# A transformer layer on one core: room of the dynamic-DMA scratch given to pages, and the copies back of the mLSTM outputs split in two

## The chip, the core and the metric

The kernel runs on one core of a Trainium2 chip. The core has a matrix engine (TensorE, in the profile PE, its weight loads PEld), a vector engine (VectorE, DVE), a scalar engine (ScalarE, ACT), GpSimd (POOL) and a sync engine (SP), which here only issues DMAs. Each engine runs its own instructions in the order in which they stand in its program; semaphores hold an instruction until what it needs is done. DMAs issued by SP and by POOL are carried out by the same 16 DMA engines. SBUF is the on-chip memory that DMAs fill and engines read; PSUM holds what PE accumulates.

The metric is the time of one execution on the device in microseconds, the median of several.

## The reference

One layer on x of 256 positions by 2048 channels: a SwiGLU feed-forward block, a mixer, a second SwiGLU block, each followed by a residual and a layer norm, then a gated embedding.

```python
x = layer_norm(ALPHA*x + 0.5*swiglu(x, ffn1_w1, ffn1_w3, ffn1_w2))        # 2048 -> 5632 -> 2048
proj = x @ w_in                                                            # 2048 x 11272
mq, mk, mv, mo, mi, mf, sq, sk, sv, ga, gb = split(proj)
y_m  = head_norm(mlstm(conv(mq), conv(mk), mv, mi, mf)) * sigmoid(mo)      # 4 heads of 256
y_sb = stick_breaking(sq, sk, sv)                                          # 8 heads of 128
merged = sigmoid(ga)*(y_m @ w_up_m) + sigmoid(gb)*(y_sb @ w_up_sb)
x = layer_norm(ALPHA*x + merged @ w_out)
x = layer_norm(ALPHA*x + 0.5*swiglu(x, ffn2_w1, ffn2_w3, ffn2_w2))
x = x + sigmoid(x @ w_ple_gate) * (p @ w_ple_proj)
```

All is float32. The weights are read once from DRAM, in blocks of 256 rows by 512 columns (0.5 MB).

## The kernel before

**Weights and units.** A block of weights is loaded from DRAM into a *raw* page (`loads`, the DMA at L1143, issued by SP). ACT then rounds it to a high part (L1170) and DVE forms the low part as the difference (L1174); both are *split* pages. A *unit* of the program multiplies one split weight with one of the two halves (t) of 128 positions: six matmuls, which are three (L1221, high by high; L1222, high by low; L1223, low by high) for each 128 rows. The left operand is an `actT` tile, activations transposed and split in the same way, one page for a chunk c of 512 channels and a half t. Some pairs of products (SwiGLU's two up-projections, the mixer's gates) are formed by `seven`, which saves one product in eight by sums of weights. Such sums are made by POOL, as DMAs that add a second block into a raw page (L337), or by DVE (L342), which needs both blocks landed. The tiles `seeded` are the PSUM banks of these products.

**Pages.** Raw blocks, splits, `actT` tiles and larger intermediates (`big`, `qk`) all live in one pool of 44 pages of 4,096 bytes per partition. A page is handed out in the order of the program; the instruction that fills it waits until the last use of what was in it is done. How far loads run ahead is limited by `limits`: in the feed-forward blocks by the count of pages in use, in the mixer by `room` (raw pages, splits), which entries of the program made by `rooms(raw, splits)` set as it goes on. The rest of SBUF is taken by constants, the residual, temporaries, and a scratch for the descriptors of dynamic DMAs, whose size the kernel leaves at its default.

**Order.** The program is a list of units and of calls, written out once; side work (transposes, softmax-like chains, normalisations) is spawned with a due time counted in matmuls, so it does not depend on pages. In the mixer, `main` (the projections q, k, v, the stick-breaking columns, then the up-projections `ups(g, 0)`) is woven with the units of the gates by `weave`. SP's queue holds all loads of weights in the order of first use, and between them the copies of the kept residual, the norms' rows, the copies back below and the outputs.

**The mLSTM outputs.** When a head pair is done, its `actT` pages (chunk c, half t) are written to DRAM by POOL (`away`, L804) and their pages given free. `back` fetches all four into new pages, by four DMAs on SP (L813). It stands in `main` four units before its end at that time, that is before the last four of the sixteen units of 256 columns which close the projections; the units of `ups(0, 0)`, from the weight `w_up_m`, come next. Of these, the first four units (two blocks of 256 rows, two halves) read chunk 0 and the next four chunk 1, with units of the gates between them.

Of the kernel before, what the change touches and what calls it, by code (L numbers as in the profile page):

```python
# [8 lines left out]
F32 = mybir.dt.float32  # L9
# [6 lines left out]
TT = S // P  # L16
# [6 lines left out]
EPS = 1e-5  # L23
COL = 512

PAGES = 44
TEMP_BUFS = 6
FORMED = 8
SPARE = 2
# [142 lines left out]
def flat(pairs):  # L172
    return [u for p in pairs for u in p]
# [7 lines left out]
def kernel(  # L181
# [6 lines left out]
    nc = tc.nc  # L188
    x, out = x[0], out[0]
# [4 lines left out]
    res_pool = ctx.enter_context(tc.tile_pool(name="res", bufs=1))  # L194
    page_pool = ctx.enter_context(tc.tile_pool(name="page", bufs=PAGES))
    temp_pool = ctx.enter_context(tc.tile_pool(name="temp", bufs=TEMP_BUFS))
# [11 lines left out]
    def temp():  # L208
        sched.until(lambda: temps[0] < TEMP_BUFS)
        temps[0] += 1  # L210
        return temp_pool.tile([P, COL], F32, name="temp", tag="temp")

    def drop(n=1):
        temps[0] -= n

    def misc(shape):
        return ps_pool.tile(shape, F32, name="ms", tag="ps")
# [6 lines left out]
    def act_tile():  # L224
        pages[0] += 1
        return page_pool.tile([P, 2, 4, P], F32R, name="actT", tag="page")
# [84 lines left out]
    def group(w, rows, col0, cols, act, done):  # L311

        accs = [{} for _ in range(TT)]
        pairs = []
        for i, r in enumerate(rows):
            tile = plain(rows_of(w, r, col0, cols))
            pairs.append([Unit(tile, t, accs[t], act, r // COL, r % COL // P,
                               i == 0, i == len(rows) - 1, done) for t in range(TT)])
        return pairs
# [68 lines left out]
    program = []  # L388

    def rooms(*n):  # L390
        return lambda: room.__setitem__(slice(0, len(n)), n)
# [5 lines left out]
    class Norm:  # L397
# [23 lines left out]
        def columns(self, raw, n):  # L421
            ps = misc([P, 2 * n])
            nc.tensor.transpose(ps[:], raw[0:2 * n, 0:P], ident[0:2 * n, 0:2 * n])
            self.gb = small.tile([P, 2, n], F32, name="gb", tag="gb", bufs=1)
            nc.vector.tensor_copy(out=self.gb[:], in_=ps.rearrange("q (a c) -> q a c", c=n))
            drop()
            return
            yield
# [307 lines left out]
    def qk_done(which, g):  # L736
        stage = {}

        def done(ps, t):
            stage[t] = temp()  # L740
            nc.scalar.copy(stage[t][:], ps)
            if t == TT - 1:
                sched.spawn(conv(which, g, stage), DELAY["cv0"])
        return done

    def conv(which, g, stage):
        yield from wait("cw")
        for e in range(2):
            h = 2 * g + e
            ps = misc([P, 2, S])  # L750
            for k in range(2):
                for t in range(TT):
                    nc.tensor.transpose(ps[:, k, t * P:(t + 1) * P],
                                        stage[t][:, (2 * e + k) * P:(2 * e + k + 1) * P], ident[:])
            if ("qk", h) not in st:
                st["qk", h] = page_pool.tile([P, 2, 2, S], F32, name="qk", tag="page")
            acc = temp().rearrange("q (k s) -> q k s", s=S)
            w = lambda k, j: st["cw"][:, j * 16 + 8 * which + 2 * h + k:j * 16 + 8 * which + 2 * h + k + 1]
            for k in range(2):
                activate(acc[:, k], ps[:, k], ACT.Copy, scale=w(k, 3))  # L760
            for k in range(2):
                for j in range(3):
                    d = 3 - j
                    nc.vector.scalar_tensor_tensor(out=acc[:, k, d:], in0=ps[:, k, :S - d], scalar=w(k, j),
                                                   in1=acc[:, k, d:], op0=ALU.mult, op1=ALU.add)
            yield DELAY["cv1"]
            activate(st["qk", h][:, which], acc[:], ACT.Silu)
            drop()
            flags.add(("qk", which, h))
            yield DELAY["cv2"]  # L770
        drop(2)
# [28 lines left out]
    ymT, ysbT = ActT(act_tile), ActT(act_tile)  # L800
    aside = {(c, t): dram_pool.tile([P, 2, 4, P], F32, name=f"aside{c}{t}") for c in range(2) for t in range(TT)}
# [4 lines left out]
        return  # L806
        yield

    def back():
        for c in range(2):  # L810
            for t in range(TT):
                ymT.tiles[c, t] = act_tile()
                nc.sync.dma_start(out=ymT.tiles[c, t][:].bitcast(F32), in_=aside[c, t][:])  # L813

    def diag(tl):
        return tl[:, 0:512].rearrange("q (a s) -> q a s", s=S)[:, :, 0:P]
# [104 lines left out]
    def in_sequence(gens):  # L921
        for g in gens:
            yield from g
            yield DELAY["m2"]
# [4 lines left out]
    head = group(w_in, range(0, D, 2 * P), 0, COL, x1T, qk_done(0, 0))  # L929
    program.extend(skewed(head[:SKEW]) + flat(head[SKEW:]))  # L930
    program.extend(columns(4096, 2 * HM + 2 * DS, gates_done))
    main = [rooms(13, 4)] + columns(1024, COL, qk_done(1, 0)) + [rooms(8)]
    main += columns(COL, COL, qk_done(0, 1)) + [load_norm_m, rooms(8)] + columns(1024 + COL, COL, qk_done(1, 1)) + [rooms(8)]
    for g in range(2):
        main += columns(2048 + g * COL, COL, v_done(g))
        main.append(lambda g=g: sched.spawn(in_sequence([mlstm(2 * g), mlstm(2 * g + 1)])))
    for first, n in ((2, 4), (8, 4), (16, 4), (12, 4), (20, 4), (6, 2)):
        main += columns(sq0 + first * DS, n * DS, lambda ps, t, f=first, n=n: sb_columns(ps, t, f, n))
        if first in (2, 20):
            main.insert(len(main) - (0 if first == 2 else 6), rooms(11 if first == 2 else 7))  # L940
        if first == 16:
            main.append(rooms(10))
            main.append(lambda: [sched.spawn(in_sequence([stick(a), stick(a + 2), stick(a + 4), stick(a + 6)]))
                                 for a in (0, 1)])

# [64 lines left out]
    def ups(g, half):  # L1010
        if half:
            return flat(group(w_up_sb, range(0, HS * DS, 2 * P), g * COL, COL, ysbT, up_done(g, 1)))
        return flat(group(w_up_m, range(0, HM * DM, 2 * P), g * COL, COL, ymT, up_done(g, 0)))

    main[len(main) - 4:len(main) - 4] = [back]
    for g in range(3):
        main += ups(g, 0) + [rooms(12)]
    program.extend(weave(main, chained([sigmoid7(w_in[:, 3072:], w_in[:, 3072 + COL:], 0, mo_place, mo_after)] + [gates7(g) for g in range(4)])))
    program.append(rooms(10, 6))
    for g in range(3):  # L1020
        program.extend(ups(g, 1))
    program.append(lambda: sched.spawn(refill(), DELAY["mt"]))
# [97 lines left out]
    def mixing():  # L1120
        j = pos["split"]
        return held[0] or any(-EDGE <= j - e < EDGE for e, _ in edges) or [m for e, m in edges if e <= j][-1:] == [True]
# [13 lines left out]
    def loads(most=len(raws)):  # L1136
        while (pos["load"] < most and pos["raw"] < (4 if pos["at"] < 6 else limits(pos["split"])[0])
               and (mixing() or pages[0] + pos["raw"] + 2 * max(limits(pos["split"])[1], len(splits)) < PAGES - SPARE)):
            j = pos["load"]
# [63 lines left out]
    for u in program:  # L1203
# [14 lines left out]
        for k in range(2):  # L1218
            hi, lo = a[:, 0, u.sub + k], a[:, 1, u.sub + k]
            first, last = u.start and k == 0, u.stop and k == 1  # L1220
# [40 lines left out]
```

## Time and profile before

| | |
|---|---|
| runs shown | 2203.69, 2204.67, 2205.21 us; median 2204.67 |
| the profiled execution | 2203.56 us, of which its span is 2201.9 |
| instructions in the span | 27807 |
| moved by DMA | 531.26 MB, mean 241 GB/s |
| granted TensorE clock, mean | 0.998 |

The span goes from the first to the last instruction of the program. The profile's page gives the busy time of each engine; its views give, for an engine or a stretch of time, the instructions in order, what ended the idle time before them, and who waited for whom. In a row of the timeline stand the start, the duration, the engine, the line of the code, the operation, the tile that is written and those that are read, and in brackets the idle time just before it with what ended that. Names with a q (SPq) are queues: their rows are the issue of a DMA. A matmul's duration overlaps the next one's, so the distance of two starts is what one costs.

### The profile page before, as it was taken

Reading aid. Unit: us, or ns where it says so; the run is one execution under the profiler, and the core shown is the slowest. Engines: PE = TensorE matmul, PEld = TensorE weight load, DVE = VectorE, ACT = ScalarE, POOL = GpSimd, SP = SyncE. Lnnn points to the kernel's source line nnn. Section 1 sums busy time; section 2 is a strip of 40 time slices with the busy share of each in tenths; the row PEclk is TensorE's granted clock in tenths of the full one; section 3 lists DMA queues with packets and bytes.
Section 4 is the critical chain, followed back from the end, with each engine's and each line's share of the span. In section 5 each row is a group of like instructions: output and inputs, shape, how many; then the busy total and the mean of one; then the engine's idle time right before and its main releaser. Section 6 shows DMA issues by size and latency. Waiting matters only on the chain.

```text
span 2201.9 us, 27807 instructions
## 1 busy us (share of the span) xinstructions
PE 2174.7 (99%) x9948; PEld 1797.7 (82%) x9948; DVE 1811.6 (82%) x1993; ACT 1345.6 (61%) x1615; POOL 242.1 (11%) x209
## 2 busy tenths in 40 slices
PE   9999999999999999999998999999999999999999
PEld 7888888888887888878886788888888888888878
DVE  6889988888898798778675877599898989889884
ACT  6556555666575666666766544556665666666562
POOL 3111001110100101011111100011011101110000
PEclk9999999999999999999999999999999999999999
DMA  9899889987993869798777876679879998999652
GB/s 347 222 254 269 255 240 303 267 246 213 287 327 116 242 186 254 216 249 262 200 212 212 301 264 196 214 167 314 260 225 248 305 258 247 245 275 302 213 166 72
DMA packets 276523, 531.26 MB, mean 241 GB/s; under 512 B 16768, under 2 KB 25888, under 8 KB 276128
## 3 DMA queue, kind: packets, MB, share of 16 engines
q1 hardware_dynamic: 229824, 437.20, 58.7%
q0 software_dynamic: 46560, 92.29, 23.0%
q8 instruction: 78, 1.28, 0.2%
q14 instruction: 61, 0.50, 0.1%
HBM read 523.12 MB, written 6.29 MB: 240 GB/s over the span
## 4 chain that ended last, share of the span: by engine, by line
PE 93%; DVE 3%; ACT 2%; issue 1%; DMA 1%; POOL 0%; DVEq 0%; ACTq 0%; POOLq 0%
PE mm L1222 25%; PE mm L1223 25%; PE mm L1221 25%; PE seeded L1222 5%; PE seeded L1221 5%; PE seeded L1223 5%; DVE split L1174 2%; PE ms L267 1%; ACT split L1170 1%; DMA actT<-aside 1%; ACT temp L239 1%; PE ms L456 0%; PE ms L848 0%; PE ms L836 0%; DVE raw L342 0%
## 5 line engine op out<-in xcount | busy, mean ns | idle before, releaser
L1174 DVE TENSOR_TENSOR split<-raw,split 128x1024 fp32r<-128x1024 f32 (+2 forms) x1073 | 1255.0, 1204 | 201.8 <-ACT split L1170 188.2
L1170 ACT CAST split<-raw 128x1024 fp32r<-128x1024 f32 (+2 forms) x1073 | 1079.2, 1038 | 463.6 <-PE mm L1222 114.8
L1221 PE MATMUL mm<-split,actT 128*128 128x512 f32 (+2 forms) x2608 | 1014.7, 389 | 9.5 <-DMA actT<-aside 6.7
L1222 PE MATMUL mm<-split,actT 128*128 128x512 f32 (+2 forms) x2608 | 1003.8, 385 | 7.2 <-DVE split L1174 7.1
L1223 PE MATMUL mm<-split,actT 128*128 128x512 f32 (+2 forms) x2608 | 1003.5, 385 | 2.3 <-DVE actT L272 2.3
L1222 PEld LDWEIGHTS mm<-split,actT 128*128 128x128 f32 x2608 | 490.7, 188 | 105.9 <-DVE split L1174 12.3
L1221 PEld LDWEIGHTS mm<-split,actT 128*128 128x128 f32 x2608 | 490.6, 188 | 105.8 <-issue 7.9
L1223 PEld LDWEIGHTS mm<-split,actT 128*128 128x128 f32 x2608 | 490.2, 188 | 100.6 <-DVE actT L272 3.1
L337 POOL DMA_DIRECT2D raw<-in_ffn_w_dram x128 | 154.7, 1216 | 1172.1 <-DVE split L1174 1016.5
L342 DVE TENSOR_TENSOR raw<-raw 128x1024 f32<-128x1024 f32 x168 | 204.6, 1218 | 22.2 <-DMA raw<-in_w_in_dram 11.7
L1221 PE MATMUL seeded<-split,actT 128*128 128x512 f32 x504 | 198.8, 394 | 0.0
L1222 PE MATMUL seeded<-split,actT 128*128 128x512 f32 x504 | 197.2, 391 | 0.2 <-DVE split L1174 0.2
L1223 PE MATMUL seeded<-split,actT 128*128 128x512 f32 x504 | 196.7, 390 | 0.0
L571 DVE SCALAR_TENSOR_TENSOR xres<-mm,xres 128x512 f32<-128x512 f32 x160 | 108.7, 684 | 22.4 <-PE mm L1223 22.4
L1222 PEld LDWEIGHTS seeded<-split,actT 128*128 128x128 f32 x504 | 95.0, 188 | 20.6 <-DVE split L1174 1.6
L1223 PEld LDWEIGHTS seeded<-split,actT 128*128 128x128 f32 x504 | 94.9, 188 | 19.8
L1221 PEld LDWEIGHTS seeded<-split,actT 128*128 128x128 f32 x504 | 95.0, 188 | 19.4 <-issue 0.3
L269 ACT CAST actT<-ms 128x512 fp32r<-128x512 f32 x60 | 35.2, 587 | 83.7 <-PE ms L267 83.7
L337 POOL DMA_DIRECT2D raw<-in_w_in_dram x40 | 48.9, 1227 | 304.1 <-DVE split L1174 241.6
L272 DVE TENSOR_TENSOR actT<-ms,actT 128x512 fp32r<-128x512 f32 x60 | 41.1, 685 | 24.2 <-ACT actT L269 15.1
L239 ACT ACTIVATE temp<-mm 128x512 f32<-128x512 f32 (+1 forms) x38 | 21.8, 574 | 57.9 <-PE mm L1223 57.9
L235 ACT ACT_TABLE_LOAD x36 | 46.2, 1283 | 0.6
(153 smaller groups left out, 714.5 us busy)
## 6 DMA issues: line engine op xcount, KB each, us to landing
raw<-in_ffn_w_dram SPq DMA_DIRECT2D x527, 512.0 KB, 8.2
raw<-in_w_in_dram SPq DMA_DIRECT2D x168, 512.0 KB, 5.4
raw<-in_ffn_w_dram POOLq DMA_DIRECT2D x128, 512.0 KB, 9.5
raw<-in_w_in_dram POOLq DMA_DIRECT2D x40, 512.0 KB, 8.5
raw<-in_w_out_dram SPq DMA_DIRECT2D x32, 512.0 KB, 4.9
raw<-in_w_ple_gate_dram SPq DMA_DIRECT2D x24, 512.0 KB, 4.9
raw<-in_w_up_m_dram SPq DMA_DIRECT2D x16, 512.0 KB, 5.7
raw<-in_w_up_sb_dram SPq DMA_DIRECT2D x16, 512.0 KB, 5.8
```

What stands on the lines that cost most here:

```text
L235: nc.scalar.preload_act_table_set(table[0])
L239: nc.scalar.activation(out, in_, func, **kw)
L269: nc.scalar.copy(dst[:, 0], ps[:])
L272: nc.vector.tensor_tensor(out=dst[:, 1], in0=ps[:], in1=dst[:, 0], op=ALU.subtract)
L337: nc.gpsimd.dma_start(out=raw.tile[:, :, :cols], in_=src.src, accum_op=ALU.add)
L342: nc.vector.tensor_tensor(out=a.tile[:, :, :cols], in0=a.tile[:, :, :cols], in1=b.tile[:, :, :cols], op=ALU.add)
L571: nc.vector.scalar_tensor_tensor(out=xs, in0=ps, scalar=0.5, in1=xs, op0=ALU.mult, op1=ALU.add)
L1170: nc.scalar.copy(hi[:, ks], r[:, ks])
L1174: nc.vector.tensor_tensor(out=lo[:, ks], in0=r[:, ks], in1=hi[:, ks], op=ALU.subtract)
L1221: nc.tensor.matmul(ps, hi, w[0][:, k, :u.cols], start=first, stop=False, skip_group_check=u.onto)
L1222: nc.tensor.matmul(ps, hi, w[1][:, k, :u.cols], start=False, stop=False, skip_group_check=u.onto)
L1223: nc.tensor.matmul(ps, lo, w[0][:, k, :u.cols], start=False, stop=last, skip_group_check=u.onto)
```

## The change

The scratch of dynamic DMAs is set to 4,096 bytes per partition, and the pool gets three pages of 4,096 bytes more. In the mixer the limits on raw pages rise: 13 to 15, 8 to 12 (twice), 8 to 11, 11 to 14, 10 to 13, 7 to 10, 12 to 15, and at its end 10 to 12. `back` fetches one chunk: chunk 0 seven units before the end of the projections, chunk 1 two units before it.

```diff
-PAGES = 44
+PAGES = 47
...
-    def back():
-        for c in range(2):
-            for t in range(TT):
-                ymT.tiles[c, t] = act_tile()
-                nc.sync.dma_start(out=ymT.tiles[c, t][:].bitcast(F32), in_=aside[c, t][:])
+    def back(c):
+        for t in range(TT):
+            ymT.tiles[c, t] = act_tile()
+            nc.sync.dma_start(out=ymT.tiles[c, t][:].bitcast(F32), in_=aside[c, t][:])
...
-    main = [rooms(13, 4)] + columns(1024, COL, qk_done(1, 0)) + [rooms(8)]
-    main += columns(COL, COL, qk_done(0, 1)) + [load_norm_m, rooms(8)] + columns(1024 + COL, COL, qk_done(1, 1)) + [rooms(8)]
+    main = [rooms(15, 4)] + columns(1024, COL, qk_done(1, 0)) + [rooms(12)]
+    main += columns(COL, COL, qk_done(0, 1)) + [load_norm_m, rooms(12)] + columns(1024 + COL, COL, qk_done(1, 1)) + [rooms(11)]
...
-            main.insert(len(main) - (0 if first == 2 else 6), rooms(11 if first == 2 else 7))
+            main.insert(len(main) - (0 if first == 2 else 6), rooms(14 if first == 2 else 10))
...
-            main.append(rooms(10))
+            main.append(rooms(13))
...
-    main[len(main) - 4:len(main) - 4] = [back]
+    for c, ahead in ((1, 2), (0, 8)):
+        main.insert(len(main) - ahead, lambda c=c: back(c))
     for g in range(3):
-        main += ups(g, 0) + [rooms(12)]
+        main += ups(g, 0) + [rooms(15)]
...
-    program.append(rooms(10, 6))
+    program.append(rooms(12, 6))
...
-    nc = bacc.Bacc("TRN2", target_bir_lowering=False, num_devices=1)
+    nc = bacc.Bacc("TRN2", target_bir_lowering=False, num_devices=1, dynamic_dma_scratch_size=4096)
```

The order of the instructions of PE, ACT, DVE and POOL is the same before and after, but for line numbers, which move by one. What moves is SP's queue. First the place where the rows of the mLSTM head norm (`in_norm_m`, L783) are loaded, among the loads of the input projection (x34 are 34 rows alike in a row):

```order
 L1143 DMA raw<-in_w_in_dram 128x2x512 x3
 L1143 DMA raw<-in_w_in_dram 128x2x264 x8
-L1143 DMA raw<-in_w_in_dram 128x2x512 x30
+L1143 DMA raw<-in_w_in_dram 128x2x512 x34
 L783 DMA big<-in_norm_m_dram 128x1024
-L1143 DMA raw<-in_w_in_dram 128x2x512 x114
+L1143 DMA raw<-in_w_in_dram 128x2x512 x110
```

Four loads of weights have moved ahead of that DMA, which itself stands at the same point of the program. Second, SP's queue around the copies back; `aside_94` and `aside_95` are the two halves of chunk 0, `aside_96` and `aside_97` those of chunk 1:

```order
 L1143 DMA raw<-in_w_up_m_dram 128x2x512 x3
 L1143 DMA raw<-in_w_in_dram 128x2x512
-L813 DMA actT<-aside_94 128x1024
-L813 DMA actT<-aside_95 128x1024
-L813 DMA actT<-aside_96 128x1024
-L813 DMA actT<-aside_97 128x1024
+L812 DMA actT<-aside_94 128x1024
+L812 DMA actT<-aside_95 128x1024
 L1143 DMA raw<-in_w_in_dram 128x2x512
 L1143 DMA raw<-in_w_up_m_dram 128x2x512 x2
+L812 DMA actT<-aside_96 128x1024
+L812 DMA actT<-aside_97 128x1024
```

Chunk 0's copies keep their place among the loads; chunk 1's now stand behind one more load of `w_in` and two more of `w_up_m`.

## The prediction

> **What bounds the kernel now.** First the busy times of the engines and the waits of the matrix engine (PE).
>
> ```profile
> PE 2174.7 (99%) x9948; PEld 1797.7 (82%) x9948; DVE 1811.6 (82%) x1993; ACT 1345.6 (61%) x1615; POOL 242.1 (11%) x209
> PE mm L1222 <- DVE split L1174: 7.1, 10, 1.1
> PE mm L1221 <- DMA actT<-aside: 6.7, 1, 6.7
> PE mm L1221 <- ACT big L1077: 2.4, 3, 1.5
> ```
>
> PE is busy for 2174.7 us of a span of 2201.9, so at most some 27 us can be had in all; an edit pays only where PE stands still or runs slowly. The last three rows give the wait in total, how often, and the longest: the ten waits for a split weight are short, and a single one, for an mLSTM output copied back from DRAM, takes 6.7 us. Next, the stretches around that wait (us from the start; then PE, PEld, DVE, ACT and POOL busy; granted clock, DMA share, GB/s).
>
> ```profile
> 1150.00:1160.00 10.00, 9.47 (x55) 7.85 (x53) 6.96 (x9) 5.99 (x9) 0.79 (x1) 1.00 0.49 131
> 1160.00:1170.00 10.00, 9.24 (x52) 7.83 (x52) 7.97 (x10) 9.08 (x12) 5.42 (x6) 1.00 0.76 144
> 1170.00:1180.00 10.00, 6.77 (x46) 5.96 (x44) 5.67 (x6) 5.28 (x8) 0.67 (x1) 1.00 1.09 255
> 1180.00:1190.00 10.00, 6.50 (x18) 5.20 (x19) 2.52 (x6) 2.37 (x4) 0.00 (x0) 0.66 0.63 237
> ```
>
> PE loses time in two ways: it waits, and from 1180 to 1190 its clock is granted at 0.66 only. The DMA engines are half idle before 1160 and full after 1170. The timelines of PE and of SP's queue there (start, duration, instruction, idle time before it and what ended that):
>
> ```profile
> 1175.95 0.82 PE L913 MATMUL ms<-temp,big 128*128 128x256 f32 x4
> 1183.50 0.76 PE L1221 MATMUL mm<-split,actT 128*128 128x512 f32 x1 [6.73 <-DMA actT<-aside]
> ...
> 1184.92 0.63 PE L1221 MATMUL mm<-split,actT 128*128 128x512 f32 x1
> 1185.34 0.63 PE L1222 MATMUL mm<-split,actT 128*128 128x512 f32 x1
> ...
> 1188.64 0.39 PE L1221 MATMUL mm<-split,actT 128*128 128x512 f32 x1
> 1188.87 0.39 PE L1222 MATMUL mm<-split,actT 128*128 128x512 f32 x1
> ...
> 1192.07 0.39 PE L1222 MATMUL mm<-split,actT 128*128 128x512 f32 x1
> ...
> 1196.53 0.47 PE L1221 MATMUL mm<-split,actT 128*128 128x512 f32 x1
> ```
> ```profile
> 1161.37 5.70 SPq L1143 DMA_DIRECT2D raw<-in_w_up_m_dram  x3
> 1170.45 0.37 SPq L1143 DMA_DIRECT2D raw<-in_w_in_dram  x1
> 1170.86 2.26 SPq L813 DMA_DIRECT2D actT<-aside  x4
> DMA to landing us min/median/max: 12.5/12.8/13.1
> ```
>
> PE is done with all else at 1176.77 (1175.95 + 0.82). The four copies back were issued only from 1170.86 on, and took 12.5 to 13.1 us to land. After the wait matmuls start 0.43 us apart, from 1188.64 on 0.23 apart: the twelve from 1183.50 to 1188.64 took 5.14 us instead of 12 x 0.23 = 2.76, so **2.4 us** were lost to the clock.
>
> **The change, part by part.** The sum is made against the profiled execution: 2203.56 us, of which 2201.9 are its span and 1.7 lie around it. It is 1.1 under the median of the three runs, 2204.67.
>
> *First pair of copies.* Three more pages, with the mixer's limits on raw pages raised by 2 to 4, let each load take the page release that served the load about three places earlier. So the w_in load ahead of the copies (1170.45) moves to about the release of 1161.37, three loads back. The first two copies follow on the next two releases, which are those of the second and third up_m load (by 1167.07, the end of that row). Issue is then 1161.4 to 1167.1, against 1170.86. Landing is bounded by the nearest rows, the up_m loads and the copies themselves:
>
> ```profile
> raw<-in_w_up_m_dram SPq DMA_DIRECT2D x6, 512.0 KB, 4.7
> raw<-in_w_in_dram POOLq DMA_DIRECT2D x4, 512.0 KB, 10.3
> ```
>
> With 4.7 us they are there by 1171.8 at the latest; with 13.1 between 1174.5 and 1180.2, and a wait of up to 3.4 is left. I take issue at 1163 to 1165 and 10 us, the figure of DMAs that share the engines with POOL's adding transfers: landed by 1175, before 1176.77. That removes **6.73** and, with no long wait, **2.4**.
>
> *Second pair.* It is recorded five mixer units later, behind three more loads (a w_in and two up_m) on SP's queue. By the same count these take the releases of 1166 to 1171 and the copies those of about 1171 to 1173, so they are issued no earlier than now. PE needs chunk 1 at the matmul now at 1196.53: less 6.73 and 2.4, at 1187.4. With 13.1 they land by 1186.1; one more load ahead of them than now costs 0.5 MB at 255 GB/s, 2.1 us, and would give 1188.2. I take no wait, with 0 to 3 as bounds. Only loads used later stand behind them on SP.
>
> *Loads earlier.* Some DVE sums of raw weights wait for a load, and PE then for the split behind them. The rows are of DVE, PE and SP:
>
> ```profile
> 840.79 1.23 DVE L342 TENSOR_TENSOR raw<-raw 128x1024 f32<-128x1024 f32 x1 [3.00 <-DMA raw<-in_w_in_dram]
> 843.21 0.50 PE L1222 MATMUL mm<-split,actT 128*128 128x512 f32 x1 [0.41 <-DVE split L1174]
> 943.77 0.50 PE L1222 MATMUL mm<-split,actT 128*128 128x512 f32 x1 [0.70 <-DVE split L1174]
> 827.64 8.30 SPq L1143 DMA_DIRECT2D raw<-in_w_in_dram  x4
> ```
>
> The load that ends the 3.00 us wait is the last of the four on SP; three places earlier is the first, at 827.64, some 8 us sooner, and 3.00 is all that is needed. The wait at 943.77 is of the same kind. Together **1.1**. The other short waits on the split are not for a load:
>
> ```profile
> 1156.46 0.87 ACT L239 ACTIVATE temp<-ms 128x384 f32<-128x384 f32 x2 [2.02 <-PE ms L889]
> 1159.53 0.50 PE L1221 MATMUL mm<-split,actT 128*128 128x512 f32 x1 [0.37 <-ACT split L1170]
> 1160.79 0.50 PE L1222 MATMUL mm<-split,actT 128*128 128x512 f32 x1 [0.76 <-DVE split L1174]
> ```
>
> Here ACT stood behind a matmul in its own order, and the orders of PE, ACT, DVE and POOL stay as they are. I count nothing; at best these and the like (7.1 in all, 1.1 counted) give 2.5 more.
>
> *What is late next.* While PE stood, ACT and DVE did not:
>
> ```profile
> 1177.96 1.04 ACT L1170 CAST split<-raw 128x1024 fp32r<-128x1024 f32 x1 [2.64 <-DMA raw<-in_w_in_dram]
> 1181.12 1.05 ACT L1170 CAST split<-raw 128x1024 fp32r<-128x1024 f32 x1
> 1188.84 1.05 ACT L1170 CAST split<-raw 128x1024 fp32r<-128x1024 f32 x1 [6.68 <-PE seeded L1223]
> 1182.20 1.23 DVE L1174 TENSOR_TENSOR split<-raw,split 128x1024 fp32r<-128x1024 f32 x1 [0.65 <-ACT split L1170]
> ```
>
> The split that DVE ends at 1183.43 feeds the matmul now at 1192.07; without wait and slow clock that one is due at 1182.9, so PE waits some **0.7** there. Behind it ACT waits for PE anyhow (6.68), so most of its work is tied to PE and shifts with it. Bounds 0 to 3.
>
> *Scratch.* POOL's DMAs keep their number, order and sizes; I take 0 for 4,096 bytes instead of 16,384 (three pages of 4,096 more). Its upper end is the slow rival below; a gain is excluded, since less room issues nothing sooner. In the two feed-forward blocks the loads come earlier too, but PE hardly waits there (the ten short waits above are nearly all in the mixer): 0.
>
> Sum: -6.73 - 2.4 - 1.1 + 0.7 = -9.5. From 2203.56 that gives 2194.0; set against the median, as a timed run will be, **2195.2**.
>
> **The rivals.**
>
> *The second pair becomes the wait.* For: it is issued as late as now, the copies' slowest landing (13.1) leaves 1.3 us, and DMA stands at 1.09 there. Against: half the copies are out of the way. If it lands 4 us late, the gain is 5.5: 2199.2. A wait as long as now's would bring the slow clock back. The Trainium skill ("TensorE: Matmul & The Clock Gate", Part 1: The HAM clock gate) says that the clock halves once an idle window of about 3.4 us has passed and needs as long a busy one to return. The trace agrees with half speed (0.43 against 0.23 us) after 6.73 us; no run here shows where the bound lies, and by that rule a residue of 4 us could cost up to 1.7 more, an estimate.
>
> *ACT and DVE become the bound from 1177 to 1210.* The lead that they built up during the wait is gone soon after:
>
> ```profile
> 1205.83 0.50 PE L1222 MATMUL mm<-split,actT 128*128 128x512 f32 x1 [0.64 <-DVE split L1174]
> ```
>
> If it is gone because they cannot keep PE's pace, the upper bound of 3 and as much again would be given back: gain 3.5 to 6.5, about 2199.7. Against it speaks that ACT waited 6.68 us for PE in this stretch.
>
> *The change does not do what it says:* the copies land no sooner because the DMA engines, not the issue, set the landing. DMA share 1.09 speaks for it, 0.49 and 0.76 before 1170 against it. Only the 1.1 is left: 2203.6.
>
> *Slower: the scratch is too small.* If it holds the descriptors of fewer adding DMAs than are in flight, POOL's next one waits for a landing, and the weights formed by it come late.
>
> ```profile
> 1161.39 1.21 POOL L337 DMA_DIRECT2D raw<-in_w_in_dram  x1 [4.68 <-DVE split L1174]
> 1164.89 2.44 POOL L337 DMA_DIRECT2D raw<-in_w_in_dram  x2 [2.29 <-DVE split L1174]
> 1168.23 1.20 POOL L337 DMA_DIRECT2D raw<-in_w_in_dram  x1 [0.90 <-DVE split L1174]
> raw<-in_ffn_w_dram POOLq DMA_DIRECT2D x128, 512.0 KB, 9.5
> raw<-in_w_in_dram POOLq DMA_DIRECT2D x40, 512.0 KB, 8.5
> q0 software_dynamic: 46560, 92.29, 23.0%
> ```
>
> Four are in flight at once (issued within 6.8 us, 10.3 to land), so room for fewer than four decides it. Then the fourth waits for the first: 1161.39 + 10.3 against 1168.23, 3.5 us. The 128 + 40 come in 21 groups of eight; with two such delays per group and, as I choose, half of them reaching PE, 21 x 3.5 = 73.5 are added to the forecast: 2268.7. Against: nothing shows that the old room was ever near full. The Trainium skill ("DMA: Bandwidth & Descriptors", Terms, and SWDGE vs HWDGE vs iDMA) puts such DMAs' descriptors, 16 bytes each, into rings in this room. By it 4,096 bytes of a partition would be 256 entries for each of 16 engines. With 46560 packets over POOL's 174 DMAs, 17 for a DMA and engine, that is room for fifteen, an estimate by which this rival falls; no run here shows a ring.
>
> **How the numbers follow.** Chances: forecast 0.64 (2193.5 to 2197.5 with the bounds above); more than forecast, the 2.5 of other waits, 0.08 (2191.5 to 2193.5); second pair 0.10; ACT and DVE 0.10; not what it says 0.04; scratch 0.04. The range 2191.3 to 2200.3 leaves out the last two, a part of the two before them, and little below. A measurement of this kernel can tell about 0.2% (4.4 us) from no change, which is 2200.3: faster 0.83, same 0.11, slower 0.06.
>
> **What would show it.** Right: no PE wait for the copies, granted clock 1.00 throughout 1170 to 1190, first copies issued near 1163 and landed before PE has done L913, no PE waits of 0.41 and 0.70 near 840 and 940, and a new short one for a split 6 us after the ups begin. Wrong: a PE wait for the copies' second pair some 10 us after the first, POOL DMA issues longer than 1.2 us or farther apart, or waits for splits spread over the feed-forward blocks.

## The result, and the profile after

| kernel | median, us | before in the same runs, us | ratio, 95% interval |
|---|---|---|---|
| the change | 2193.43 | 2205.21 | 0.9946 [0.993, 0.9962] |
| the change, run again | 2192.6 | 2204.45 | 0.9945 [0.9932, 0.9957] |

The change makes the kernel faster by 0.54%, some 11.8 us. The forecast was 2195.2 with a range of 2191.3 to 2200.3, so the time is 1.8 us under it and inside. The first profile of the change fell in a disturbed execution (a span of 5668.4 us), and so did the first of the copies in two steps alone (2711.3 us), so for each of these two kernels the profile of its second run is read. That of the change has a span of 2192.1 us, 9.8 under before's 2201.9.

First the busy times and the waits of PE (total, times, longest):

```profile
PE 2171.4 (99%) x9948; PEld 1796.5 (82%) x9948; DVE 1810.8 (83%) x1993; ACT 1343.5 (61%) x1615; POOL 242.7 (11%) x209
PE mm L1222 <- DVE split L1174: 5.8, 7, 1.1
PE ms L824 <- DVE actT L262: 1.0, 1, 1.0
PE mm L1221 <- ACT temp L667: 0.6, 1, 0.6
```

The row of 6.7 us for `actT<-aside` is gone. What is left are short waits, and two of them are new: 1.0 us for a transposed tile and 0.6 us for a copy out of PSUM (L667). The first of the two is not in the profile of the run with a scratch of 2,048 bytes below, which differs from the change in that number alone, so it need not be there in every execution. The stretches around the copies (busy times, clock, DMA share, GB/s as before):

```profile
1160.00:1170.00 10.00, 10.00 (x64) 8.75 (x64) 8.43 (x10) 8.77 (x12) 4.88 (x5) 1.00 1.05 268
1170.00:1180.00 10.00, 9.14 (x46) 7.22 (x45) 4.52 (x5) 3.10 (x6) 0.00 (x0) 1.00 1.09 272
1180.00:1190.00 10.00, 9.20 (x43) 7.27 (x43) 8.40 (x11) 8.18 (x13) 1.23 (x1) 1.00 0.70 247
```

From 1170 to 1190 PE is busy for 18.3 us instead of 13.3, and the granted clock is 1.00 throughout. The DMA engines are full from 1160 on (1.05); before, they were only from 1170 on (0.76 and then 1.09). The timelines of PE and of SP's queue:

```profile
1173.41 0.82 PE L912 MATMUL ms<-temp,big 128*128 128x256 f32 x4
1174.81 0.51 PE L1221 MATMUL mm<-split,actT 128*128 128x512 f32 x1 [0.58 <-ACT temp L667]
...
1179.73 0.50 PE L1222 MATMUL seeded<-split,actT 128*128 128x512 f32 x1 [0.28 <-DVE split L1174]
...
1181.64 0.49 PE L1221 MATMUL mm<-split,actT 128*128 128x512 f32 x1
1182.90 0.50 PE L1222 MATMUL mm<-split,actT 128*128 128x512 f32 x1 [0.77 <-DVE split L1174]
1183.23 0.39 PE L1223 MATMUL mm<-split,actT 128*128 128x512 f32 x1
1183.46 0.40 PE L1221 MATMUL mm<-split,actT 128*128 128x512 f32 x1
...
1187.47 0.47 PE L1221 MATMUL mm<-split,actT 128*128 128x512 f32 x1
```
```profile
1158.81 0.37 SPq L1143 DMA_DIRECT2D raw<-in_w_in_dram  x1
1160.27 1.28 SPq L812 DMA_DIRECT2D actT<-aside  x2
...
1169.79 0.84 SPq L812 DMA_DIRECT2D actT<-aside  x2
DMA to landing us min/median/max: 6.7/10.9/13.6
```

PE comes to the up-projections at 1174.23 (1173.41 + 0.82) instead of 1176.77. Its first matmul there starts at 1174.81 instead of 1183.50, and the one that reads chunk 1 (1187.47, before at 1196.53) waits for nothing. The first pair of copies is issued at 1160.27, the second at 1169.79; at the longest landing of the four, 13.6 us, the second pair is there by 1183.9.

Since PE's order is the same in all these kernels, the start of the same matmul can be set side by side. (DVE's order is not quite the same, other than said with the change: near 1139 and 1147 the change forms a sum of raw weights one split sooner than before does. What that is worth was not separated.) Below, the start in each profiled kernel less that in before, in us, worked out from the PE timelines; the experiments behind the four right-hand columns follow.

| start in before | change | copies in two steps alone | pages alone | change with old limits | five splits from the ups on |
|---|---|---|---|---|---|
| 499.98 | 0.34 | 0.80 | 0.73 | 0.59 | 0.87 |
| 669.91 | -0.42 | 0.80 | -0.04 | -0.18 | 0.11 |
| 900.11 | -1.74 | 0.72 | -1.34 | 2.79 | -1.19 |
| 976.09 | -3.06 | 0.53 | -2.66 | 1.47 | -2.51 |
| 1067.99 | -2.12 | 0.58 | -2.65 | 1.49 | -2.44 |
| 1175.95 | -2.54 | 1.38 | -3.07 | 1.72 | -2.86 |
| 1183.50 | -8.69 | -5.20 | -2.17 | -4.88 | -9.35 |
| 1188.64 | -10.94 | -7.48 | -2.06 | -7.16 | -11.63 |
| 1196.53 | -9.06 | -5.51 | -1.78 | -5.17 | -9.46 |
| 1240.89 | -9.01 | -5.47 | -1.75 | -5.18 | -12.71 |
| 2189.96 | -9.80 | -5.44 | -2.53 | -5.95 | -13.45 |

Read down the second column: 2.5 us are won before the up-projections, 6.5 within them (up to 1196.53), 0.7 after. The first row, some 0.3 to 0.9, is the start of the program, which differs by that much from one execution to the next.

### The profile page after: what moved, and what is told of

Its sections match the earlier page's. It is cut to its first block, busy times and chain, and to the rows that moved or that the text cites. A ratio compares the mean times of both kernels' runs of the same rounds, so it can differ in the third digit from the quotient of the medians.

```text
span 5668.4 us, 27832 instructions
## 1 busy us (share of the span) xinstructions
PE 5662.0 (100%) x9948; PEld 3412.1 (60%) x9948; DVE 1870.2 (33%) x1993; ACT 1353.6 (24%) x1615; POOL 232.6 (4%) x209
## 4 chain that ended last, share of the span: by engine, by line
PE 100%; DVE 0%; ACT 0%; issue 0%
PE mm L1221 27%; PE mm L1223 27%; PE mm L1222 27%; PE seeded L1221 5%; PE seeded L1222 5%; PE seeded L1223 5%; PE ms L267 1%; PE ms L456 1%; PE ms L888 0%; PE ms L901 0%; PE ms L835 0%; PE ms L912 0%; PE ms L847 0%; PE ms L673 0%; PE ms L753 0%; PE ms L824 0%
## 5 line engine op out<-in xcount | busy, mean ns | idle before, releaser
L1221 PE MATMUL mm<-split,actT 128*128 128x512 f32 (+2 forms) x2608 | 2147.7, 823 | 0.0
L1223 PE MATMUL mm<-split,actT 128*128 128x512 f32 (+2 forms) x2608 | 2120.9, 813 | 0.0
L1222 PE MATMUL mm<-split,actT 128*128 128x512 f32 (+2 forms) x2608 | 2119.9, 813 | 0.0
L1174 DVE TENSOR_TENSOR split<-raw,split 128x1024 fp32r<-128x1024 f32 (+2 forms) x1073 | 1277.8, 1206 | 1907.7 <-ACT split L1170 1321.3
L1223 PEld LDWEIGHTS mm<-split,actT 128*128 128x128 f32 x2608 | 926.5, 355 | 599.8 <-issue 598.6
L1222 PEld LDWEIGHTS mm<-split,actT 128*128 128x128 f32 x2608 | 930.9, 357 | 579.0 <-issue 567.0
L1221 PEld LDWEIGHTS mm<-split,actT 128*128 128x128 f32 x2608 | 924.0, 354 | 586.7 <-issue 564.6
L1221 PE MATMUL seeded<-split,actT 128*128 128x512 f32 x504 | 422.5, 838 | 0.0
L1223 PE MATMUL seeded<-split,actT 128*128 128x512 f32 x504 | 417.0, 827 | 0.0
L1222 PE MATMUL seeded<-split,actT 128*128 128x512 f32 x504 | 416.8, 827 | 0.0
L1223 PEld LDWEIGHTS seeded<-split,actT 128*128 128x128 f32 x504 | 177.2, 352 | 123.1 <-issue 122.9
L1221 PEld LDWEIGHTS seeded<-split,actT 128*128 128x128 f32 x504 | 179.3, 356 | 118.8 <-issue 115.5
L1222 PEld LDWEIGHTS seeded<-split,actT 128*128 128x128 f32 x504 | 177.7, 353 | 115.1 <-issue 113.6
L267 PE MATMUL ms<-ident,temp 128*128 128x128 f32 x176 | 62.9, 537 | 0.0
```

What stands on the lines that cost most here:

```text
L267: nc.tensor.transpose(ps[:, k], src[:, k * P:(k + 1) * P], ident[:])
L1174: nc.vector.tensor_tensor(out=lo[:, ks], in0=r[:, ks], in1=hi[:, ks], op=ALU.subtract)
L1221: nc.tensor.matmul(ps, hi, w[0][:, k, :u.cols], start=first, stop=False, skip_group_check=u.onto)
L1222: nc.tensor.matmul(ps, hi, w[1][:, k, :u.cols], start=False, stop=False, skip_group_check=u.onto)
L1223: nc.tensor.matmul(ps, lo, w[0][:, k, :u.cols], start=False, stop=last, skip_group_check=u.onto)
```

## The experiments

The theories to be told apart: that the first pair of copies comes sooner because of the three pages and the raised limits (as the prediction had it), or because `back(0)` is recorded at an earlier place; and that the smaller scratch costs nothing, or costs something that the pages pay for.

### The change once more

The kernel is the changed one, unaltered.

> The change once more, for a profile that can be read beside the one of before. Forecast's theory: about 2193 us again; no PE wait for actT<-aside (6.7 before), granted clock 1.00 from 1160 to 1190, the first copies back issued near 1163 (1170.9 before), the two waits near 842 and 943 (0.41 and 0.70) gone, one new wait of about 0.7 for a split some 6 us after the up-projections begin. The rival that ACT and DVE become the bound expects new split waits of 3 us or more in all between 1175 and 1215. The profile taken of the change had matmuls 0.58 us apart instead of 0.23 over the whole program: if the kernel causes that, it comes again here in some execution; if not, all executions stay near 2193.

Measured: 2192.6 us, ratio 0.9945 [0.9932, 0.9957]; the profile is the one above.

### The scratch alone

```diff
-    nc = bacc.Bacc("TRN2", target_bir_lowering=False, num_devices=1)
+    nc = bacc.Bacc("TRN2", target_bir_lowering=False, num_devices=1, dynamic_dma_scratch_size=4096)
```

This is the kernel before, with 44 pages, and nothing else changed.

> The kernel before with only the scratch at 4,096 bytes (44 pages). The profile of the change has four waits of POOL before its adding DMAs that no instruction ended, 20.7 us in all, against 0.3 before; at 1,024 bytes there were 74, 455.5 us. If the room causes them they come here too, 15 to 25 us on POOL; none of them reached PE in the change, so the time stays within 0.1% of before (2203 to 2206). If they come from the pages or the limits, POOL waits 0.3 us here.

Measured: 2204.8 us, ratio 1.0001 [0.9992, 1.0009]. The wait of PE for the copies is what it was:

```profile
PE mm L1221 <- DMA actT<-aside: 6.6, 1, 6.6
```

POOL has no wait by "issue" before an adding DMA here. So 4,096 bytes cost nothing, and by themselves bring nothing.

### Where the scratch does begin to cost

Both are the change with a smaller number.

```diff
-    nc = bacc.Bacc("TRN2", target_bir_lowering=False, num_devices=1, dynamic_dma_scratch_size=4096)
+    nc = bacc.Bacc("TRN2", target_bir_lowering=False, num_devices=1, dynamic_dma_scratch_size=1024)
```
and 2048 in place of 1024.

> The change with the scratch at 1,024 bytes, a quarter again. Four of POOL's adding DMAs are in flight at once in the trace of before. If room is a limit as the slow rival had it, POOL's issues (1.2 us each) get longer or farther apart, waits for splits appear in the feed-forward blocks, and the time is 20 us or more above the change's 2193; if nothing waits for room, 2193 within 0.2%. If room is short but the splits' lead over PE (2 to 4 us) takes it up, POOL's issues get longer and the time stays within 5 us.

> The change with a scratch of 2,048 bytes. If what counts is how many adding DMAs find room at once, the POOL waits lie between the 4 of 4,096 bytes and the 74 of 1,024, and the time between 2193 and 2392 us, nearer the lower end (2195 to 2240) if three or four fit, since four was the most in flight before. If 1,024 hit a fixed cost of another kind, 2193.

Measured: with 1,024 bytes 2391.68 us, ratio 1.0853 [1.0837, 1.087]; with 2,048 bytes 2193.16 us, 0.9947 [0.9934, 0.9961], which is the change's own time. First POOL's and PE's waits with 1,024 bytes, and one of POOL's adding DMAs there:

```profile
POOL raw L337 <- issue: 455.5, 74, 8.8
PE seeded L1221 <- DVE seeded L525: 49.7, 11, 6.5
...
253.13 1.21 POOL L337 DMA_DIRECT2D raw<-in_ffn_w_dram  x1 [6.98 <-issue]
```

POOL stands 455.5 us in 74 waits that nothing in the profile ends ("issue"). Set against the landings, 168 of POOL's 174 DMAs start with no other in flight, and 141 of them 0.2 to 0.45 us after the one before has landed. No two adding DMAs are ever in flight at once (the six others all have a copy away, L804, among them): there is room for one. PE then waits for what the sums feed. With 2,048 bytes the same view has

```profile
220.62 1.22 POOL L337 DMA_DIRECT2D raw<-in_ffn_w_dram  x1 [1.14 <-issue]
```

and it starts 0.31 us after the landing of the third DMA before it, as fourteen others do within 0.26 to 0.32. Never are more than three adding DMAs in flight: there is room for three. (Three of the 174 start with three others in flight, of which two each time are copies away.) So one adding DMA of 0.5 MB takes more than 512 bytes of a partition (two do not fit in 1,024) and at most 683 (three fit in 2,048); 4,096 would hold six or seven, an estimate, where before and the change both have at most four in flight.

### The copies in two steps alone

The kernel before, with its 44 pages, limits and scratch, and `back` as in the change:

```diff
-    main[len(main) - 4:len(main) - 4] = [back]
+    for c, ahead in ((1, 2), (0, 8)):
+        main.insert(len(main) - ahead, lambda c=c: back(c))
```

> The kernel before with only the copies back in two steps (44 pages, old limits, old scratch). Theory A (the place in the program where the copies are recorded sets when they are issued): first pair issued near 1163, the 6.7 us wait and the slow clock (2.4) gone, some 8 to 9.5 us faster than before, about 2196. Theory B (as the prediction put it: the three pages and the raised limits bring the copies forward): without them the copies are issued at about 1170.9 as before, the wait stays at 5 us or more, and the time is within 2 us of before, about 2204.

> The split of the copies alone once more, for a profile at full clock. It gained 6.4 us where theory A had 8 to 9.5. Either the second pair (recorded two units before the end, behind three loads) lands after PE needs it, then PE waits some 2 us for actT<-aside about 10 us after the up-projections begin; or the first pair still comes late, then the wait stands where it stood, shorter than 6.7; or neither, and the splits behind the wait are late: new waits for split of 2 to 3 us in all between 1176 and 1215.

Measured: 2198.03 us, ratio 0.9968 [0.9956, 0.998]; again 2198.12, 0.9971 [0.9959, 0.9983]. SP's queue in the second run:

```profile
1161.91 0.37 SPq L1143 DMA_DIRECT2D raw<-in_w_up_m_dram  x1
1163.37 0.89 SPq L812 DMA_DIRECT2D actT<-aside  x2
DMA to landing us min/median/max: 7.6/8.8/10.0
```

Without one page more the first pair is issued at 1163.37 instead of 1170.86, has landed by 1173.8, and PE does not wait for it. The copies now stand behind one `w_up_m` load where before had three and a `w_in` load. The loads themselves come no sooner: that `w_in` load is at 1171.44 here and at 1170.45 before. What is missing of the 8 to 9.5 us of theory A are new short waits for a split, the third of the three cases: 0.55, 0.37 and 0.76 us (before the matmuls at 1175.18, 1183.28 and 1186.45).

### The pages alone

The change with both pairs recorded where before had them:

```diff
-    for c, ahead in ((1, 2), (0, 8)):
-        main.insert(len(main) - ahead, lambda c=c: back(c))
+    main[len(main) - 4:len(main) - 4] = [lambda: back(0), lambda: back(1)]
```

> The change with all four copies back at the old place, four units before the end of the projections (47 pages, raised limits, scratch of 4,096). Theory A: copies issued near 1170.9, three loads more ahead of them, a PE wait for actT<-aside of about 6 us and the slow clock stay; only the load waits (1.1) and up to 2.5 more of other split waits go, so 2201.5 to 2204. Theory B: copies issued at 1161 to 1167, no such wait, 2194 to 2197.

Measured: 2199.95 us, ratio 0.9979 [0.997, 0.9988]. SP's queue, the copies' landing, and PE's wait (line numbers of loads and matmuls are one lower in this kernel):

```profile
1158.29 4.89 SPq L1142 DMA_DIRECT2D raw<-in_w_in_dram  x2
1163.63 4.17 SPq L1142 DMA_DIRECT2D raw<-in_w_up_m_dram  x2
1167.85 2.02 SPq L812 DMA_DIRECT2D actT<-aside  x4
DMA to landing us min/median/max: 14.0/14.7/15.5
PE mm L1220 <- DMA actT<-aside: 7.6, 1, 7.6
```

With three more pages and the raised limits the loads come sooner (the `w_in` load that was at 1170.45 is the first of the two at 1158.29), and more of them run ahead: one more of `w_in` and two more of `w_up_m` are in the queue ahead of the copies. These come only 3 us sooner and take longer to land. PE, which is 3.07 us ahead here, waits 7.6 instead of 6.7, and the clock falls again (0.85 from 1170 to 1180, 0.64 from 1180 to 1190). What remains at 1196.53 is 1.78.

### The old limits on the new pages

The change with `rooms` as before (13, 8, 8, 8, 11, 10, 7, 12, and 10 at the end):

```diff
-    main = [rooms(15, 4)] + columns(1024, COL, qk_done(1, 0)) + [rooms(12)]
+    main = [rooms(13, 4)] + columns(1024, COL, qk_done(1, 0)) + [rooms(8)]
...
```

> The change with the mixer's old limits on raw pages (13, 8, 8, 8, 11, 10, 7, 12, 10); 47 pages, scratch of 4,096 and the split copies stay. If the three pages alone give the loads their lead (a page handed out was given back longer ago), the time is that of the change, 2192 to 2194. If the limits do, the loads of the mixer keep most of their lateness: the waits of 0.41 and 0.70 near 842 and 943 come back in part and the time is 1 to 4 us above the change, 2194 to 2197; the copies are issued as early as in the change either way.

Measured: 2194.87 us, ratio 0.9956 [0.9943, 0.997]. The pages without the limits lose at one place what the limits win there, on PE:

```profile
844.95 0.78 PE L1222 MATMUL mm<-split,actT 128*128 128x512 f32 x1 [2.36 <-DVE split L1174]
...
845.96 0.63 PE L1221 MATMUL mm<-split,actT 128*128 128x512 f32 x1
846.38 0.63 PE L1222 MATMUL mm<-split,actT 128*128 128x512 f32 x1
...
848.48 0.39 PE L1221 MATMUL seeded<-split,actT 128*128 128x512 f32 x1
```

The wait that was 0.41 before and is none in the change is 2.36 here, and from 844.95 to 848.48 matmuls start 0.43 us apart: the clock is halved. The sum on DVE that feeds this split waited 5.32 us for its load, where before's waited 3.00; why that load came later still was not followed. In SP's queue the copies stand where the place alone put them:

```profile
842.54 1.23 DVE L342 TENSOR_TENSOR raw<-raw 128x1024 f32<-128x1024 f32 x1 [5.32 <-DMA raw<-in_w_in_dram]
1162.79 0.99 SPq L812 DMA_DIRECT2D actT<-aside  x2
1171.50 0.37 SPq L1143 DMA_DIRECT2D raw<-in_w_in_dram  x1
```

The `w_in` load is at 1171.50, after the first copies and no sooner than before: it is the raised limits that let the loads run ahead there, and 47 pages without them do not. The copies come in time all the same, so their term rests on the place and not on the limits. In the median this kernel is some 2 us slower than the change, with intervals that overlap; the execution in the profile is the slowest of its five (2197.62 us, the others 2194.14 to 2196.59), so the table's column for it shows more loss than the median.

### Five splits in place of two raw pages

The short waits for a split that are left at the up-projections suggested a page more for splits. Three variants of the change have it. The first, from the last projections on:

```diff
-            main.insert(len(main) - (0 if first == 2 else 6), rooms(14 if first == 2 else 10))
+            main.insert(len(main) - (0 if first == 2 else 6), *([rooms(14)] if first == 2 else [rooms(8, 5)]))
...
-        main += ups(g, 0) + [rooms(15)]
+        main += ups(g, 0) + [rooms(13, 5)]
```

> The change with one more split weight ahead (5 instead of 4) and two raw pages fewer (8 instead of 10, 13 instead of 15) from the last projections to the first part of the up-projections. In the change PE waits there for splits in short steps (0.35, 0.76, 0.58, 0.28, 0.77, 0.64, 0.75 us between 1157 and 1231) since ACT stands behind a matmul in its own order. If the splits' lead of four is what is short, half or more of these 4 us go: 2189.5 to 2191.5. If ACT's order behind PE sets them whatever the lead, 2193 as the change; if the raw pages given up were needed, waits for loads return and it is 1 to 3 us slower.

The second, from the middle of the mixer on, where every later limit on raw pages is lower by 1 or 2:

```diff
-    main = [rooms(15, 4)] + columns(1024, COL, qk_done(1, 0)) + [rooms(12)]
+    main = [rooms(13, 5)] + columns(1024, COL, qk_done(1, 0)) + [rooms(10)]
...
-        main += ups(g, 0) + [rooms(15)]
+        main += ups(g, 0) + [rooms(13)]
```

> The same exchange (5 splits, two raw pages fewer) over the whole mixer up to the second part of the up-projections. If the lead is short everywhere in the mixer, 2187 to 2191; if two raw pages fewer bring back late loads near 842 and 943, as the old limits did (one wait of 2.36 us with 3.4 us of slow clock), 2194 to 2197.

The third, from the up-projections on:

```diff
+    main.append(rooms(9, 5))
     for g in range(3):
-        main += ups(g, 0) + [rooms(15)]
+        main += ups(g, 0) + [rooms(13, 5)]
```

> The change with five splits (raw pages 9, then 13) only from the up-projections on, at the end of the projections; the stretch of the last projections keeps its limits of the change (10 raw, 4 splits). The theory says that the change's short waits of PE for a split from 1174 to 1231 us (0.28, 0.77, 0.64, 0.75, some 2.4 in all) come from having only four splits at the up-projections, and that the wait of 3.73 us which five splits left in the version with five from the last projections on came from casts of ACT that were put earlier than the adding DMAs of POOL they need. Then the waits of 1156 to 1158 us (0.35 and 0.76) are there again as in the change, the later ones are gone, and no wait of 3.73 us for the copy out of PSUM stands near 1172: 2190.5 (2189.5 to 2191.5). The rival says that the fifth split sets off the same wait wherever it comes (ACT behind POOL's adding DMAs at the head of the up-projections): then a wait of 2 to 4 us with the slow clock behind it stays, and the time is 2192 to 2194, no better than the change.

| five splits | median, us | ratio, 95% interval | span of the profile, us |
|---|---|---|---|
| from the last projections on | 2190.78 | 0.9939 [0.9926, 0.9951] | 2190.0 |
| from the middle on | 2192.57 | 0.9946 [0.9932, 0.9959] | 2191.8 |
| from the up-projections on | 2190.03 | 0.9934 [0.9916, 0.9952] | 2188.4 |

With five splits from the last projections on, the short waits near 1157 are gone, but PE has one of 3.7 us. It and ACT's order around it:

```profile
PE mm L1221 <- ACT temp L667: 3.7, 1, 3.7
...
1170.31 1.04 ACT L1170 CAST split<-raw 128x1024 fp32r<-128x1024 f32 x1 [2.75 <-DMA raw<-in_w_in_dram]
1174.35 1.04 ACT L1170 CAST split<-raw 128x1024 fp32r<-128x1024 f32 x1 [2.99 <-DMA raw<-in_w_in_dram]
1175.30 0.64 ACT L667 COPY temp<-mm 128x256 f32<-128x256 f32 x2
```

The fifth split lets ACT reach casts whose sums POOL's DMAs have not yet formed; ACT waits 2.75 and 2.99 us for them in its order, and the copy that frees PE's bank stands behind. PE's clock is halved for 3.4 us after that wait. Begun at the up-projections, one such cast fewer stands ahead of that copy (lines one higher here):

```profile
1172.79 1.04 ACT L1171 CAST split<-raw 128x1024 fp32r<-128x1024 f32 x1 [2.79 <-DMA raw<-in_w_in_dram]
1173.74 0.64 ACT L667 COPY temp<-mm 128x256 f32<-128x256 f32 x2
```

There PE waits 0.2 us for the copy. This is the fastest kernel of the study, 14.3 us under before's 2204.32 in the same runs. Its place in the table of starts shows the gain of 3.7 over the change: 0.4 up to 1196.53 and 3.3 from there to 1240.89, where the change still has three short waits (0.64, 0.21 and 0.75), worth some 2.4 at the price that is worked out below; the rest was not followed. One wait for a split that should have gone stayed (0.76 us, before the matmul at 1182.11). From the middle on there is a wait of 4.1 us for the copy, and one of 1.6 at 977 that is shown at the end. Against the change, which ran at another time, its interval overlaps; the order of the medians is what the starts bear out.

## Why the prediction was right, and where it was not

**First pair of copies (-6.73): the size was right, the cause only in part.** The wait is gone, and the copies were issued at 1160.27, somewhat before the 1163 to 1165 that the prediction took. They landed after 6.7 and 9.0 us; the 10 that it took for this came from a row of POOL's adding DMAs themselves. The step "Three more pages, with the mixer's limits on raw pages raised by 2 to 4, let each load take the page release that served the load about three places earlier" is right for the loads: the `w_in` load ahead of the copies goes from 1170.45 to 1158.81. But it does not carry the copies. With pages and limits alone three more loads get ahead of them, they come at 1167.85, and PE waits longer; with the place alone the loads about keep their times, three fewer stand ahead of the copies, they come at 1163.37, and PE does not wait. The mistake was to take from the order that "Chunk 0's copies keep their place among the loads" and to leave the earlier recorded place out of the account. The order is the product of two shifts that cancel in it: the raised limits put three loads ahead of the copies, the earlier place takes as many away.

**Slow clock (-2.4): right.** The start of the same matmul goes from -8.69 to -10.94 between 1183.50 and 1188.64, 2.25 us.

**Second pair (0): right.** It was issued at 1169.79, a little before the 1171 to 1173 foreseen, landed by 1183.9 and was needed at 1187.47, against a forecast of 1187.4. Some 3.6 us were to spare, so the rival by which it becomes the wait falls.

**Loads earlier (-1.1): the sign right, the term too small.** From 669.91 to 976.09 the start moves by 2.64. One reason is that a wait costs more than its row says. Of the change's rows above, 1181.64 to 1183.46 are three matmuls in 1.82 us; undisturbed ones take 3 x 0.23 = 0.69, so the wait of 0.77 cost 1.13. Part of the difference is that the idle time is counted from the modelled end of the matmul before: 0.39 of duration less the 0.23 at which the next one could start is 0.16. Before's rows of a wait in the first feed-forward block say the same:

```profile
580.98 0.39 PE L1221 MATMUL mm<-split,actT 128*128 128x512 f32 x1
581.79 0.50 PE L1222 MATMUL mm<-split,actT 128*128 128x512 f32 x1 [0.43 <-DVE split L1174]
...
582.38 0.40 PE L1221 MATMUL mm<-split,actT 128*128 128x512 f32 x1
```

Here it is 1.40 instead of 0.69, 0.71 for a row of 0.43. So the two waits of 0.41 and 0.70 were worth some 1.7, not 1.1. Most of what then remains comes in three steps of 0.2 to 0.3 near 857, 867 and 954, where before has no wait long enough for a row of its own. After 976 the new wait of 1.0 us for `actT` (the row L824 above) gives 0.94 back, and 0.4 more are won by 1175.95.

**The feed-forward blocks (0): wrong by 1.5.** The wait just shown is gone, and so is one like it near 1972 in the second block: 0.8 each (0.34 to -0.42, and -9.01 to -9.80). The run with the old limits gains as much at both places, so this comes from the pages. Waits that are "nearly all in the mixer" are not all.

**What is late next (+0.7): right in place, too small in sum.** The wait for the split was foreseen at 1182.9 and is there, at 1182.90, with 0.77. Not foreseen were 0.58 for the copy L667 and 0.28 for a split at 1179.73. From 1175.95 to 1196.53 the start moves by 6.52, against 6.73 + 2.4 - 0.7 = 8.43: 2.6 were given back, not 0.7. This lies within the bounds of 0 to 3, and short of the rival's 3 and as much again. The two last terms, the loads and the feed-forward blocks too small and what is late too small as well, stand against each other, which is why the sum of 9.5 comes near the 9.8 of the spans: that nearness is luck. The measured 2193.43 stands just under the 2193.5 at which the forecast's own range ended and the rival of more than forecast began, and part of what that rival named, other short waits, did go.

**Scratch (0): right, the rival's point and price wrong.** There, "room for fewer than four decides it". With room for three, the case that it priced at 73.5 us, nothing is lost: POOL starts 15 DMAs just behind a landing, and PE does not feel it. With room for one the loss is 2391.68 - 2192.6 = 199 us. The estimate of room for fifteen in 4,096 bytes, 17 descriptors of 16 bytes for a DMA and engine, is not borne out: 272 bytes each, where the runs give 512 to 683. The Trainium skill ("Collectives: The Full Stack", Part 3, The bandwidth ceiling) says of the adds that the DMA engines do in a collective that they take one descriptor for each of two sources. By that it would be 2 x 17 x 16 = 544 bytes, an estimate that lies within the measured bounds. In the change POOL has four waits by "issue" too, of 6.45, 3.93, 6.43 and 3.91 us. They are not for room: at the same DMAs before waited 6.10, 3.69, 5.98 and 3.69 for a split.

**The parts together.** In the medians the place alone brings 6.5 us (2198.12 against 2204.57), the pages with their limits alone 4.5 (2199.95 against 2204.45), and both 11.9. The sum, 11.0, is within what such medians can tell of it. In the last row of the table of starts it is 5.4, 2.5 and 9.8, some 1.8 more for both than for the parts, and the starts say where that comes from. About 0.8 is the wait for a split at 1175.18 in the run with the place alone, which neither of the other two has. Some 0.9 lies in the stretch of the copies (1175.95 to 1196.53), where both together win 6.5 and the place alone 6.9, while the pages alone lose 1.3: there PE is 3.07 ahead and has 1.78 left, since the copies that it waits for let it start only 2.17 sooner and the clock is slow for longer (10.2 us instead of 6.8). Only with the copies early is that lead kept.

## What to carry to other kernels

Where a DMA stands in an in-order queue behind loads that run ahead, letting these run further ahead may put more of them in front of it; record it earlier, and test the place and the buffers apart even where the order reads the same. Time won ahead of a transfer that PE must wait for is lost in that wait, so remove the last long wait first and then look for the short ones. Count a short wait by the starts of the matmuls around it, not by its own row: here it cost some 0.3 us more.

## What was not expected of the hardware

**Waits of 2.36 and 1.61 us halved the clock.** After the 2.36 us in the run with the old limits it was half for 3.4 us, as the rows above show. In the run with five splits from the middle on, 1.61 us were enough:

```profile
976.82 0.40 PE L1223 MATMUL mm<-split,actT 128*128 128x512 f32 x1
978.83 0.69 PE L824 MATMUL ms<-big 4*128 4x256 f32 x2 [1.61 <-DVE actT L262]
...
980.67 0.63 PE L1222 MATMUL mm<-split,actT 128*128 128x512 f32 x1
981.10 0.63 PE L1223 MATMUL mm<-split,actT 128*128 128x512 f32 x1
...
983.66 0.40 PE L1221 MATMUL mm<-split,actT 128*128 128x512 f32 x1
```

The clock fell 1.4 us after the wait had ended and came back by 983.66; together with the wait this cost 3.1 us (the start against before goes from -2.68 to 0.45). It is not the length alone, since a wait of 1.69 us in the change left the clock at 1.00:

```profile
31.83 0.50 PE L1223 MATMUL mm<-split,actT 128*128 128x512 f32 x1 [1.69 <-DVE actT L272]
32.17 0.40 PE L1221 MATMUL mm<-split,actT 128*128 128x512 f32 x1
32.40 0.39 PE L1222 MATMUL mm<-split,actT 128*128 128x512 f32 x1
```

When the clock changes, the traces do show: only on a grid of 3.413 us. In the run with five splits from the middle on it falls at 980.25 and 1178.23 and returns at 983.67 and 1181.64, so the stretches are 3.41, 194.56 and 3.41, which is 1, 57 and 1 times 3.413; with the pages alone the slow stretch of 10.24 is three times that. The change's clock is recorded as 1.00 from 4.74 to 2192.68, 641 times 3.413, so its grid is known too. Below, the windows of this grid that hold the three waits, for the old limits, five splits from the middle on and the change (length, then busy times, clock, DMA share and GB/s):

```profile
841.59:845.00 3.41, 1.05 (x6) 0.55 (x4) 2.46 (x3) 1.04 (x1) 0.00 (x0) 1.00 1.09 281
976.84:980.25 3.41, 1.80 (x7) 0.96 (x6) 2.27 (x4) 2.86 (x7) 0.00 (x0) 1.00 1.07 300
28.63:32.05 3.42, 1.73 (x8) 1.13 (x7) 3.40 (x6) 3.08 (x4) 1.34 (x1) 1.00 1.05 386
```

Each of the three waits lies wholly in one window, and the clock falls, where it does, at that window's end.

The Trainium skill ("TensorE: Matmul & The Clock Gate", Part 1: The HAM clock gate) speaks of a free-running window of about 3.4 us and of one idle window. The grid agrees with the first; the windows before the two falls were not idle, since PE was busy in them for 1.05 and 1.80 us. PE's busy time alone does not settle it either, with 1.73 in the window after which the clock stayed. Of the 1.80, some 0.7 are the two matmuls of L824 that use only 4 rows of the array; that such work counts for less would fit, but no run here tests it.

**The room of an adding DMA** is 512 to 683 bytes of a partition of the scratch, and while there is room for three at a time this kernel loses nothing.
